# Softmax attention: probabilities scaled in place and transposed, instead of multiplied with a diagonal matrix

## The chip, the cores and the metric

The kernel runs on one core of one Trainium2 chip, as one program. The metric is device microseconds of one execution. A core has five engines that each run their instructions in order and meet only through semaphores: PE (matrix products, with PEld for the load of the stationary operand), DVE and ACT (elementwise work, reductions, functions, and copies out of PSUM), POOL, and SP, which here issues the transfers from memory.

## The reference, cut to what matters

Two layers of a first block and two of a second one, on 512 tokens of width 1024, in 32-bit floats. The first block has four groups of four heads: softmax attention with forget gates (fox), latent attention (mla), stick-breaking attention, and a sliding window of 128 keys (swa). The second has eight heads of softmax attention over keys that an indexer picks (dsa), and two recurrent groups (rwkv, gdn). Each block also has dense projections and feed-forwards of width 2816. What the change touches is the same in fox, mla, swa and dsa:

```
s = jnp.einsum('bqhd,bkhd->bhqk', qi, k).astype(jnp.float32) * scale
...
p = jax.nn.softmax(s, axis=-1).astype(v.dtype)
return jnp.einsum('bhqk,bkhd->bqhd', p, v)
```

## The kernel before

Features lie on the 128 partitions and the 512 tokens along the free dimension (`x` is eight tiles of 128x512). Dense products run as three products of split 32-bit numbers (`mm3`: high times high, high times low, low times high, in the type float32r). Weights come by SP, are split by ACT (line 235) and by DVE or POOL (line 236), and stream through PE.

Attention works on pairs of heads and tiles of 128 queries. `pair` (line 641) is one query tile `i` of two heads, in stages separated by `yield`:

- the scores go to PSUM (`sc`); DVE adds the bias and takes the row's extreme in one pass (line 654), which gives the tile `p` in SBUF, 128 queries by n*128 keys. n is 1 to 4 for fox, mla and dsa, and 1 or 2 for swa;
- ACT takes the exponential in place and adds up the row (line 665);
- DVE takes one over the row's sum (line 672), and the identity is multiplied by it, per partition, into a 128x128 tile `dg` (line 674, through `lin`). For head 0 in the first block (site `dg0`, listed in `ACT`) that is ACT at line 107, for head 1 there and for both heads in the second block DVE at line 109;
- PE multiplies each 128x128 block of `p`, as the stationary operand, with `dg` (line 681, through `mm`, line 164). This turns the block and divides it by the row's sum at once. The results lie in PSUM (`pt`) and are copied to SBUF (`pT`, line 682);
- PE multiplies the values with `pT` into `ot`, and ACT copies that out (lines 687 and 688).

There are 24 such pairs in each layer of the first block (8 each of swa, fox and mla) and 16 in each layer of the second. Per layer they have, over both heads, 108 blocks of 128x128 in the first block (28 swa, 40 fox, 40 mla) and 80 in the second: 376 in the whole kernel.

The order on PE is written ahead of time by `weave`: each stream (a pair, a recurrence, the projections as filling) yields an estimate of PE time until its next stage can start, and the stream that has been ready longest is written next. The clock of this planner, `self.t`, grows by an estimate for each product: in `mm` 4/2400 us for each column of a 32-bit float (0.213 us for 128 columns), in `tr` 0.21 us for a transpose. Three pairs are in flight at a time (`L1`, `L2`). The transposes of the kernel before, such as those of the dsa queries (`qqp`) and of the recurrences' matrices (`iXT`), go through `tr`, line 168.

Of the kernel before, what the change touches and what calls it, by code (L numbers as in the profile page):

```python
# [17 lines left out]
T = 512  # L18
D = 1024
# [47 lines left out]
class Ctx:  # L67
# [36 lines left out]
    def lin(self, site, out, x, scale, bias=0.0):  # L104
        """out = x scale + bias"""
        if site in ACT:
            self.nc.scalar.activation(out, x, AF.Identity, scale=scale, bias=bias)
        elif isinstance(bias, float) and bias == 0.0:
            self.nc.vector.tensor_scalar(out, x, scale, None, op0=OP.mult)
        else:  # L110
            self.nc.vector.tensor_scalar(out, x, scale, bias, op0=OP.mult, op1=OP.add)
# [5 lines left out]
    # interleaved emission ------------------------------------------------------------  # L117
    # A stream is a generator. It yields the tensor engine's time (us) until its next stage can start, or a key
    # that some other stream announces with done or hit. Engines run in order, so the streams are merged by
    # this clock: the stage that has been ready for longest comes next, and fill streams where none is ready.  # L120
# [30 lines left out]
    @staticmethod  # L151
    def lanes(gens, n):
        """n streams that share the generators of a list in order"""
        it = iter(gens)

        def lane():
            for g in it:
                yield from g
        return [lane() for _ in range(n)]
# [10 lines left out]
    # tiles ---------------------------------------------------------------------------  # L170
# [15 lines left out]
    def tables(self, k):  # L186
        """loads the activation engine's set of functions k, here in its order"""
# [20 lines left out]
    def split(self, src, name, w=T, gain=None):  # L208
        """hi + lo == src (times gain) exactly, both exact in float32r"""
# [10 lines left out]
    # dense products ------------------------------------------------------------------  # L220
    def weight(self, src, nk, m, name="w", eng=None, slots=False):
        """split weights [(hi, lo)] of nk k tiles [128, m]; slots: in the tiles of S instead of the weights' own"""
# [27 lines left out]
    def dense(self, jobs, head=0, ws=()):  # L250
        """jobs (weights, k tiles, columns, run(split weights)) in order, the weights ahead; ws = first split weights"""
# [9 lines left out]
    def tjob(self, src, nk, m, xs, fin, wait=None, name="pj"):  # L261
        """fin(psum [m, 512]) of weights^T times the transposed stream"""
# [13 lines left out]
    def kjobs(self, src, ncol, tiles, xs, fin):  # L276
        """token-major projections of at most four token tiles: x stationary, weights moving"""
# [19 lines left out]
    def part(self, E, p):  # L297
        """announces part p of the mixed features; project takes them in this order"""
        E["parts"].append(p)
        self.done.add("part%d" % len(E["parts"]))  # L300

    def heads(self, wgu):
        """the first weights of the next feed-forward, ahead of time"""
        self.head = {f: self.gateup(wgu, f) for f in range(HEAD)}

    def lead(self, srcs, nk, m, name, more=False):
        """the first weights of the next projections, ahead of time"""
# [6 lines left out]
    def project(self, E, src, xd, parts, scale, st, mean, last, wgu):  # L314
        """x = scale x + (mixed features)^T w, part by part: parts[p] = first k tile, splits(); last(j) when x[j] is done"""
# [27 lines left out]
    def gemmx(self, a, b, w, xs):  # L343
        """weights^T times a presplit stream: tokens of the first half to a, second half, gains and biases to b"""
# [4 lines left out]
    def unpack(self, a, b, eng, name):  # L349
        """the products of gemmx: tile [128, 512] and columns g W, b W"""  # L350
# [20 lines left out]
    # norms ---------------------------------------------------------------------------  # L371
    def sums(self, st, x, j, mean=True):
        """running sums over the feature tiles of the transposed stream (or of some of its tokens)"""
# [17 lines left out]
    def colstats(self, st, mean, tag="d"):  # L391
        """per token tile columns: mean square [, mean]"""
# [7 lines left out]
    def rows(self, col, ps=None):  # L400
        """[128 tok, n] -> PSUM [128, n * 128], every partition the row over tokens"""
# [6 lines left out]
    def hcol(self, sqs, col):  # L408
        """sums of squares over the two heads of each tile: PSUM [128 tok, 8 per tile = 4 token tiles x 2]"""
# [6 lines left out]
    def hrows(self, m, i):  # L416
        """columns of tile i -> PSUM [128 = 2 heads x 64, 512 tok]"""
# [7 lines left out]
    def rsqrt(self, y, a, scale=1.0):  # L425
        """y = scale / sqrt(a) for small tiles: Newton from an estimate in the bits of the float"""
# [10 lines left out]
    def rs_col(self, ps, eps, w):  # L437
        """1 / sqrt(ps + eps)"""
# [5 lines left out]
    # LayerNorm(x) W = r (x g) W - r mean (g W) + b W: the first products run on (x g) and take r and the mean later.  # L444
    def lngain(self, gcol, bcol, f=None):
        """g and the splits [128, 8, 4] of g and b per feature tile (hi, hi, lo, lo), all times f"""
# [14 lines left out]
    def presplit(self, x, j, gains):  # L461
        """the split of x g, with the gains and biases as two more columns"""
# [9 lines left out]
    def unfold(self, t, rows, m):  # L472
        """t (x g) W -> LayerNorm(x) W in place; m = columns g W, b W"""
# [7 lines left out]
    def lnrows(self, st):  # L481
        """rows r and -mean r over the tokens, in two steps"""
# [15 lines left out]
    def ln(self, x, rows, gcol, bcol, split, each=None):  # L498
        """LayerNorm over features of x (in place), split if asked for; each(x[j], j) as they come. In steps."""
# [26 lines left out]
    def gnorm(self, ts, n, gcols, name, out):  # L526
        """rms norm of a group of n features held transposed in the tiles ts; out gets the splits"""
# [21 lines left out]
    def swiglu(self, xs, wgu, wdn, evac, stats, ahead, finish=None, npre=0):  # L549
        """evac(half, j, psum) takes tile j of the halves of the down projection. stats = steps to the rows of the norm;  # L550
        with finish, xs is presplit, and finish(rows) -> split of the normalized stream, the steps of its own rows or
        None. The steps of the norm go between the first products."""
# [87 lines left out]
    # softmax attention ---------------------------------------------------------------  # L640
    def pair(self, wait, score, vget, bias, i, first, out, fin, sinks=None, dg="dg", pt="pT", pace=PACE1):
        """query tile i of two heads -> out [128 = 2 x 64 dv, 128 q] in SBUF, from softmax of -(negs + bias).
        score(h, i, first, n, ps) fills the negated logits; vget(h, key tile) -> [128 keys, 64]."""
# [23 lines left out]
        ds = []  # L667
        for h in range(2):
            m = ms[h]
# [3 lines left out]
            d = self.S("dg", w=128)  # L673
            self.lin(dg + str(h), d, self.ident, m[:, 2:3])
            ds.append(d)
        yield pace[2]
        pts = []
        for h in range(2):
            t = self.P("pt", w=w)
            for j in range(n):  # L680
                self.mm(t[:, j * 128:(j + 1) * 128], ps[h][:, j * 128:(j + 1) * 128], ds[h])
# [9 lines left out]
    # block 1 -------------------------------------------------------------------------  # L691
# [31 lines left out]
    def block1(self, l, x, xs, pre, a):  # L723
        """pre: None or presplit stream before its norm, its sums, finish(rows) -> x, xs"""
# [301 lines left out]
    # block 2 ------------------------------------------------------------------------  # L1026
    def rms(self, st, tag="d", rtag="o"):
        """1/rms per token, in two steps: per token tile [128, 4], and broadcast over partitions [128, 512]"""
# [4 lines left out]
    def ffn(self, x, xs, st, wgu, wdn, gnext, ahead, finish=None):  # L1033
        """x + swiglu(rms norm of x) / 2 from its split and its sums; the split for the next gains, and the sums"""
# [12 lines left out]
    # delta rules: units u = (pair, chunk, head of the pair); chunks of 128 tokens --------  # L1047
# [11 lines left out]
    def diag16(self, X, n, Y):  # L1059
        """X: 4 tiles [128, 4 units, 128], strictly upper; the list Y gets tiles with (I - X)^-1 of the 16 x 16  # L1060
        diagonal blocks, zero elsewhere."""
# [25 lines left out]
    def merges(self, X, Y, RH, fin):  # L1087
        """Y from inverses of diagonal 16 blocks to (I - X)^-1 for the 4 units of X [128, 4, 128];
        fin takes [128, 2 chunks, (u | w) x 2 heads x 64] = inverse times the right-hand side RH"""
# [60 lines left out]
    def gram(self, p, cp, lts, rts, outs):  # L1150
        """outs[m] [128 s, 4 units, 128 t] = lts[m]^T rts[m] per head and chunk of the pair p, chunks 2cp, 2cp+1,
        each given as (destination [128, 4, 128], factor [128, 4, 128] or [128, 128])"""
# [14 lines left out]
    def tokmajor(self, srcs, p, cp):  # L1167
        """transposes of the pair tiles' chunks 2cp, 2cp+1: PSUM [128 tok, src, chunk, 128 (2 heads x 64)]"""
# [7 lines left out]
    def step(self, ch, St, UW, kd, M, dst, qg, ediag, fscale, extra=None):  # L1176
        """outputs of chunk ch (over qg's columns, in place) and the next block-diagonal state St[0].
        UW [128, 256] = u (2 heads x 64) | w (2 heads x 64); kd [128, 128]; M(e) [128 s, 128 t]"""
# [52 lines left out]
    def rwkv(self, l, vec, E):  # L1231
        """projected tiles r0..r6 = wl, r, r, k, k, v, v, each [128, 513] with a zero column first."""
# [219 lines left out]
    def gdn(self, l, vec, E):  # L1452
        """projected tiles g0..g5 = q q k k v v [128, 515] with 3 zero columns first; z0, z1; ba [128 tok, 4, 8]."""
# [31 lines left out]
        def rowpair(name, p, k):  # L1485
            """row k (0: summed gates, 1: beta) of the pair's heads: [128 = 2 heads x 64, 512 tok]"""
# [155 lines left out]
    # sparse attention -------------------------------------------------------------------  # L1642
    def rope(self, x, ct, st, nh, out, tag):
        """token-major rotation of [128, nh, 64]; ct, st [128, 64]."""
# [11 lines left out]
    def headnorm(self, x, nh, scale):  # L1656
        """[128, nh] of scale / rms over each head of 64."""
# [10 lines left out]
    def stacked(self, src, name, out):  # L1668
        """[128 tok, 8 heads, 64] -> two float32r tiles [128 = hi 64 | lo 64, 4 heads, 128 tok]"""
# [68 lines left out]
    def logits(self, ps, q, g, n):  # L1738
        """two float32r passes over [hi; lo] stacked queries: q [128, 128], keys of head g"""
# [206 lines left out]
def pack_t(w, nk):  # L1946
    """[K, N] -> [N/128, 128, nk*128] with feature k*128 + p on partition p."""
# [4 lines left out]
def pack_dn(w):  # L1952
    """[F, D] -> [2, 8, 128, 11*128]"""
# [214 lines left out]
```

## Time and profile before

| what | value |
|---|---|
| three runs | 3784.54, 3784.54 and 3778.14 us; median 3784.54 us |
| profiled execution, first to last instruction | 3779.7 us; what lies around it is not shown |
| PE busy in it | 3683.6 us (97%) |
| DVE, ACT, POOL busy | 2093.9 us (55%), 1439.4 us (38%), 288.5 us (8%) |
| mean granted clock of PE | 0.987 of full speed |
| products into `pt`: PE records, summed busy time | 752, 100.5 us |

PE's records overlap, and their ends are modelled, so the summed busy time of PE is more than the time it takes; what an instruction costs is read from one start to the next. POOL's spans are rough. Attention of the first block lies at about 31 to 285 us and 731 to 985 us of the span, the dsa pairs at about 2066 to 2150 us and 3266 to 3350 us. What lies between is mostly feed-forwards.

### The profile page before, as it was taken

The numbers are of one execution on the slowest core, as the hardware profiler recorded it, in microseconds if no ns is written. First come the engines' busy times: TensorE is split into PE (matmuls) and PEld (weight loads), VectorE is DVE, ScalarE is ACT, GpSimd is POOL, SyncE is SP. The second block draws the span as 40 slices with busy tenths as digits, with TensorE's granted clock in tenths as the row PEclk, the third lists the DMA queues.
The fourth block names the chain that finished last, engine by engine and source line by source line (L and its number), as shares of the span: only waits on it lengthen the run. The fifth ranks groups of instructions, "written<-read, shape, count | busy, mean of one in ns | idle before, by whom it ended". The sixth has DMA issues, their size and how long they took to land.

```text
span 3779.7 us, 49398 instructions
## 1 busy us (share of the span) xinstructions
PE 3683.6 (97%) x19004; PEld 2980.8 (79%) x19004; DVE 2093.9 (55%) x4405; ACT 1439.4 (38%) x2706; POOL 288.5 (8%) x294
## 2 busy tenths in 40 slices
PE   9999999999999999999998999999999999899999
PEld 7777888777788888888786878888888777688887
DVE  5378333647653357345699564444444678855343
ACT  5455222545442235223443542233223433543222
POOL 1111000111200000001212000000000211100000
PEclk9999999999999999999998999999999999899999
DMA  3113232211223232324212132323233321213332
GB/s 127 47 57 102 84 106 86 94 61 48 86 88 98 88 96 88 102 87 144 76 54 65 39 101 85 105 87 99 85 103 99 95 69 50 79 33 102 95 95 89
DMA packets 146843, 320.72 MB, mean 85 GB/s; under 512 B 31496, under 2 KB 57768, under 8 KB 146352
## 3 DMA queue, kind: packets, MB, share of 16 engines
q1 hardware_dynamic: 146608, 317.57, 27.3%
q8 instruction: 149, 2.44, 0.3%
q14 instruction: 86, 0.70, 0.1%
HBM read 301.74 MB, written 15.78 MB: 84 GB/s over the span
## 4 chain that ended last, share of the span: by engine, by line
PE 87%; DVE 9%; ACT 1%; issue 1%; DMA 1%; POOL 0%; DVEq 0%; ACTq 0%; POOLq 0%
PE gup L164 37%; PE dn L164 19%; PE pjp L164 6%; PE wop L164 3%; PE tp L164 3%; PE pt L164 2%; PE sc L164 2%; PE ot L164 1%; PE gux L164 1%; PE iY L164 1%; PE G L164 1%; PE iR L164 1%; DVE isc L1778 1%; PE rowp L164 1%; PE sb L164 1%
## 5 line engine op out<-in xcount | busy, mean ns | idle before, releaser
L164 PE MATMUL dn<-hh,downl 128*128 128x512 f32 x1056 | 416.5, 394 | 0.0
L164 PE MATMUL dn<-hh,downh 128*128 128x512 f32 x1056 | 416.0, 394 | 0.0
L164 PE MATMUL dn<-hl,downh 128*128 128x512 f32 x1056 | 415.8, 394 | 0.0
L164 PE MATMUL gup<-xsh,gh 128*128 128x512 f32 x976 | 385.3, 395 | 0.7 <-ACT xsh L216 0.6
L164 PE MATMUL gup<-xsl,gh 128*128 128x512 f32 x976 | 385.3, 395 | 0.2 <-DVE xsl L217 0.2
L164 PE MATMUL gup<-xsl,uh 128*128 128x512 f32 x976 | 385.1, 395 | 0.0
L164 PE MATMUL gup<-xsh,uh 128*128 128x512 f32 x976 | 384.8, 394 | 0.0
L164 PE MATMUL gup<-xsh,ul 128*128 128x512 f32 x976 | 384.6, 394 | 0.0
L164 PE MATMUL gup<-xsh,gl 128*128 128x512 f32 x976 | 384.6, 394 | 0.0
L235 ACT CAST downh<-down 128x768 fp32r<-128x768 f32 x192 | 150.0, 782 | 518.6 <-PE dn L164 316.2
L597 DVE TENSOR_TENSOR hh<-gup,silu 128x512 f32<-128x512 f32 x122 | 84.4, 692 | 398.8 <-PE gup L164 393.2
L235 ACT CAST gh<-g 128x1024 fp32r<-128x1024 f32 (+1 forms) x138 | 139.2, 1013 | 415.2 <-issue 325.8
L236 DVE TENSOR_TENSOR downl<-down,downh 128x768 fp32r<-128x768 f32 x192 | 171.3, 893 | 217.7 <-ACT downh L235 216.6
L235 ACT CAST uh<-u 128x1024 fp32r<-128x1024 f32 (+1 forms) x138 | 139.4, 1012 | 354.9 <-PE gup L164 319.7
L236 DVE TENSOR_TENSOR ul<-u,uh 128x1024 fp32r<-128x1024 f32 (+1 forms) x138 | 162.3, 1178 | 152.3 <-ACT uh L235 148.4
L164 PEld LDWEIGHTS dn<-hl,downh 128*128 128x128 f32 x1056 | 198.3, 188 | 47.1
L164 PEld LDWEIGHTS dn<-hh,downl 128*128 128x128 f32 x1056 | 198.2, 188 | 46.7
L164 PEld LDWEIGHTS dn<-hh,downh 128*128 128x128 f32 x1056 | 198.3, 188 | 46.4
L164 PEld LDWEIGHTS gup<-xsh,gh 128*128 128x128 f32 x976 | 183.3, 188 | 44.7 <-ACT xsh L216 1.7
L164 PEld LDWEIGHTS gup<-xsl,gh 128*128 128x128 f32 x976 | 183.3, 188 | 44.5 <-DVE xsl L217 1.2
L164 PEld LDWEIGHTS gup<-xsh,uh 128*128 128x128 f32 x976 | 183.3, 188 | 43.5
L164 PEld LDWEIGHTS gup<-xsh,ul 128*128 128x128 f32 x976 | 183.3, 188 | 43.1
(595 smaller groups left out, 7473.3 us busy)
## 6 DMA issues: line engine op xcount, KB each, us to landing
g<-in_w_gu_dram SPq DMA_DIRECT2D x132, 512.0 KB, 3.5
u<-in_w_gu_dram SPq DMA_DIRECT2D x132, 512.0 KB, 3.5
down<-in_w_dn_dram SPq DMA_DIRECT2D x96, 384.0 KB, 3.1
pj<-in_w_in_dram SPq DMA_DIRECT2D x62, 512.0 KB, 3.7
down<-in_w_dn_dram SPq DMA_DIRECT2D x96, 320.0 KB, 2.9
wo<-in_w_o_dram SPq DMA_DIRECT2D x96, 128.0 KB, 2.2
xd<-x SPq DMA_DIRECT2D x24, 256.0 KB, 2.0
x<-xd SPq DMA_DIRECT2D x24, 256.0 KB, 5.0
```

The costliest lines, as they stand in the source:

```text
L164: self.nc.tensor.matmul(out, l, r, start=start, stop=stop)
L235: nc.scalar.copy(hi, r)
L236: (eng or nc.vector).tensor_sub(lo, r, hi.bitcast(F32))
L597: nc.vector.tensor_mul(hh, u, s)
L1778: nc.vector.match_replace(acc, m8, acc, -2.0 * BIG)
```

## The change

The 128x128 diagonal is no longer made. Instead the probabilities themselves, 128 by n*128, are multiplied by one over their row's sum, in place, by the same engine that made the diagonal. PE then transposes each block with the identity. The copies, the products with the values and the sites that choose the engines stay. The diff also takes comments and docstrings out of the file; all else of it is here:

```
         yield pace[1]
-        ds = []
         for h in range(2):
-            m = ms[h]
+            m, p = ms[h], ps[h]
             if sinks is not None:
                 nc.vector.tensor_add(m[:, 1:2], m[:, 1:2], m[:, 3:4])
             nc.vector.reciprocal(m[:, 2:3], m[:, 1:2])
-            d = self.S("dg", w=128)
-            self.lin(dg + str(h), d, self.ident, m[:, 2:3])
-            ds.append(d)
+            self.lin(dg + str(h), p, p, m[:, 2:3])
         yield pace[2]
         pts = []
         for h in range(2):
             t = self.P("pt", w=w)
             for j in range(n):
-                self.mm(t[:, j * 128:(j + 1) * 128], ps[h][:, j * 128:(j + 1) * 128], ds[h])
+                self.tr(t[:, j * 128:(j + 1) * 128], ps[h][:, j * 128:(j + 1) * 128])
             pts.append(self.evac(t, "a" if h == 0 else self.o(pt), name="pT"))
```

## Rows read from the trace of the kernel before

**Rows 1.** The page: busy time per engine, then the chain that ended last.

```profile
PE 3683.6 (97%) x19004; PEld 2980.8 (79%) x19004; DVE 2093.9 (55%) x4405; ACT 1439.4 (38%) x2706; POOL 288.5 (8%) x294
...
PE 87%; DVE 9%; ACT 1%; issue 1%; DMA 1%; POOL 0%; DVEq 0%; ACTq 0%; POOLq 0%
```

**Rows 2.** Windows: window, us, busy us per engine (x instructions), PEclk, DMA share, GB/s.

```profile
31.00:80.00 49.00, 47.61 (x311) 38.71 (x310) 28.90 (x132) 27.98 (x88) 4.77 (x2) 1.00 0.11 33
130.00:200.00 70.00, 70.00 (x401) 49.97 (x401) 37.76 (x114) 38.34 (x107) 8.53 (x11) 1.00 0.04 12
200.00:285.00 85.00, 83.44 (x486) 62.42 (x485) 63.63 (x172) 49.91 (x137) 13.29 (x20) 1.00 0.21 63
...
2066.00:2092.00 26.00, 24.99 (x165) 20.13 (x164) 23.27 (x101) 17.99 (x67) 3.45 (x3) 1.00 0.49 147
2092.00:2165.00 73.00, 73.00 (x656) 63.85 (x656) 33.06 (x101) 41.48 (x107) 1.27 (x1) 1.00 0.11 32
```

**Rows 3.** The same windows, instructions on the tile pt alone.

```profile
31.00:80.00 49.00, 7.56 (x56) 7.17 (x56) 3.11 (x8) 2.74 (x8) 1.00 0.11 33
130.00:200.00 70.00, 10.69 (x80) 9.78 (x80) 3.93 (x8) 3.34 (x8) 1.00 0.04 12
200.00:285.00 85.00, 10.26 (x80) 10.10 (x80) 3.78 (x8) 3.39 (x8) 1.00 0.21 63
...
2066.00:2092.00 26.00, 6.88 (x48) 6.15 (x49) 0.00 (x0) 4.39 (x16) 1.00 0.49 147
2092.00:2165.00 73.00, 14.38 (x112) 13.31 (x112) 0.00 (x0) 8.44 (x17) 1.00 0.11 32
```

**Rows 4.** Groups by form: into pt, into iXT, copies out: busy us, mean ns | idle before.

```profile
L164 PE MATMUL pt<-dg,p 128*128 128x128 f32 x752 | 100.5, 280 | 3.8 <-DVE dg L109 3.3 <-ACT pT L194 0.4
...
L168 PE MATMUL iXT<-cs,X 128*128 128x128 f32 x64 | 8.4, 275 | 0.0
...
L194 ACT COPY pT<-pt 128x512 f32<-128x512 f32 x24 | 13.9, 581 | 10.6 <-PE pt L164 10.5
...
L194 ACT COPY iXT<-iXT 128x512 f32<-128x512 f32 x16 | 8.6, 595 | 0.1
```

**Rows 5.** Timeline of PE, clock 1.00: start us, us, instruction, xcount.

```profile
2097.24 1.50 PE L164 MATMUL pt<-dg,p 128*128 128x128 f32 x12
2098.58 1.47 PE L168 MATMUL iXT<-cs,X 128*128 128x128 f32 x12
2099.89 0.84 PE L164 MATMUL pt<-dg,p 128*128 128x128 f32 x6
```

**Rows 6.** ACT groups by form: the diagonal, and exponentials with one value a partition.

```profile
L665 ACT ACTIVATE p<-p,m 128x256 f32<-128x256 f32 x56 | 28.0, 500 | 5.3 <-DVE m L654 5.2
...
L665 ACT ACTIVATE p<-p,m 128x512 f32<-128x512 f32 x32 | 23.1, 722 | 10.8 <-DVE m L654 10.7
...
L107 ACT ACTIVATE dg<-cs,m 128x128 f32<-128x128 f32 x48 | 18.0, 395 | 0.5 <-DVE m L672 0.5
```

**Rows 7.** DVE, tiles dg and kk: duration ns min/median/max of a multiplication.

```profile
L109 DVE TENSOR_SCALAR dg<-cs,m x112: 266/283/1135, 37.0 to 3339.1; 128x128 f32<-128x128 f32 x112
L109 DVE TENSOR_SCALAR kk<-sh,vec x4: 486/961/1436, 1818.1 to 3010.6; 128x512 f32<-128x512 f32 x4
```

**Rows 8.** Waits of PE over the span: waited for, us in total, times, longest us.

```profile
PE pt L164 <- DVE dg L109: 3.3, 5, 1.2
```

**Rows 9.** Timeline of PE around the transposes of the queries, second layer.

```profile
3259.26 0.63 PE L164 MATMUL wop<-mxh,woh 128*128 128x512 f32 x1
3259.68 3.38 PE L168 MATMUL qqp<-cs,qqs 128*128 128x128 f32 x16
3262.82 0.48 PE L164 MATMUL wop<-mxl,woh 128*128 128x512 f32 x1
...
3264.02 2.12 PE L168 MATMUL qqp<-cs,qqs 128*128 128x128 f32 x16 [0.27 <-ACT qqt L194]
3265.97 0.50 PE L164 MATMUL sc<-kst,qqt 128*128 128x256 f32 x2
```

**Rows 10.** Windows there: all engines, then PEclk.

```profile
3252.50:3255.90 3.40, 1.34 (x6) 0.75 (x4) 3.40 (x28) 1.11 (x3) 1.74 (x2) 0.99 0.01 2
3255.90:3259.20 3.30, 1.39 (x3) 1.16 (x4) 3.30 (x12) 0.72 (x3) 1.59 (x2) 0.50 0.00 0
3259.20:3262.60 3.40, 3.40 (x16) 2.96 (x15) 3.24 (x12) 0.71 (x2) 1.68 (x1) 0.50 0.00 0
3262.80:3266.00 3.20, 2.93 (x23) 2.19 (x21) 2.58 (x9) 3.20 (x8) 0.00 (x0) 1.00 0.78 259
```

More of the change, by code (lines that the diff above doesn't have):

```diff
@@ L666, in pair @@
         yield pace[1]
-        ds = []
         for h in range(2):
-            m = ms[h]
+            m, p = ms[h], ps[h]
             if sinks is not None:
@@ L672, in pair @@
             nc.vector.reciprocal(m[:, 2:3], m[:, 1:2])
-            d = self.S("dg", w=128)
-            self.lin(dg + str(h), d, self.ident, m[:, 2:3])
-            ds.append(d)
+            self.lin(dg + str(h), p, p, m[:, 2:3])
         yield pace[2]
@@ L680, in pair @@
             for j in range(n):
-                self.mm(t[:, j * 128:(j + 1) * 128], ps[h][:, j * 128:(j + 1) * 128], ds[h])
+                self.tr(t[:, j * 128:(j + 1) * 128], ps[h][:, j * 128:(j + 1) * 128])
             pts.append(self.evac(t, "a" if h == 0 else self.o(pt), name="pT"))
```

## The prediction

> **What bounds the kernel now.** I read the page first: PE is busy 97% of the span, and 87% of the chain that ended last runs through PE [rows 1]. That is an average over unlike stages, so the next view is the windows in which the pairs lie. PE fills the windows 130 to 200 us and 2092 to 2165 us without a gap; it has 1.4 us free of 49 in the first attention window and 1.6 of 85 in the third. In the first dsa window it has 1.0 free of 26, but there DVE is busy for 23.3 us of 26 and PE follows it [rows 2]. The windows of the other layers (731 to 985 us and 3266 to 3365 us) repeat these five. Then I looked at whether PE ever stands still for the thing that changes: over the whole span it waits for a finished diagonal 3.3 us, in 5 places [rows 8]. So the diagonals are nearly always early, and what counts is what the products themselves take on PE.
>
> **What one block costs on PE, before and after.** The busy times of PE's groups overlap (280 ns a product's record, 275 ns a transpose's [rows 4]), and by them the two cost the same. Two other readings say otherwise. One is the number of records: the code has 376 blocks, and `pt` has 752 matmul records, two for each block; `iXT` goes through `tr`, its 16 copies of 512 columns make 64 blocks of 128, and it has 64 records, one for each [rows 4]. A product of plain 32-bit floats is run as two passes and a transpose as one. The other is the distance of starts, where 12 records of each kind stand side by side at full clock: the 12 of `pt` take 2098.58 - 2097.24 = 1.34 us, 112 ns each, and the 12 transposes 2099.89 - 2098.58 = 1.31 us, 109 ns each [rows 5]. A block costs 2 x 112 = 224 ns as a product and 109 ns as a transpose of the same 32-bit type. The saving is 115 ns a block, 376 x 0.115 = 43.2 us. By stretch, with half the records of [rows 3] as blocks: 28, 40 and 40 blocks in the three windows of the first block (3.2, 4.6 and 4.6 us), 24 and 56 in the two of the second (2.8 and 6.4 us), each twice.
>
> **What is added.** The reciprocal is multiplied into 128 to 512 columns where it was into 128. On ACT (48 times) a multiplication of 128 columns takes 395 ns. For wider ones I take the exponentials, which have the same form: 500 ns for 256, 722 ns for 512 and the middle, 611 ns, for 384 [rows 6]. With 12, 20, 8 and 8 of the four widths that is 20 x 0.105 + 8 x 0.216 + 8 x 0.327 = 6.4 us. On DVE (112 times) 128 columns take 283 ns in the median, and the same operation on 512 columns takes 486 ns at its shortest [rows 7], so 68 ns for each further block: 20 x 0.068 + 8 x 0.135 + 8 x 0.203 = 4.1 us in the first block, and 16 x (0.068 + 0.135 + 0.203) = 6.5 us in the second, where both heads use DVE. These 17 us lie on engines that are half to three fifths busy in three of the five windows, in front of products that hardly ever wait. From below the price on the path is nothing (the cover is other work on PE). From above, with all cover gone, it is the longer of the two engines for each pair: 6.4 us in the first block and 6.5 us in the second, 13 us. I take 1.5 us, near the lower end because of the 3.3 us of [rows 8]: 0.5 us in each first dsa window, where DVE is full and 8 multiplications have one block more, and 0.5 us elsewhere. The diagonals' tiles fall away, which frees small tiles and costs nothing. Behind a longer multiplication on ACT stand exponentials and copies of other pairs, on DVE also the splits of weights. That is the same cover, in the same bound.
>
> **How much of the saving stays.** The order on PE is fixed in advance, and the planner takes 0.21 us for a transpose and took 0.213 us for a product. So the order stays almost as it is, while a transpose really takes 109 ns. Wherever one pair's blocks were to cover another pair's wait, up to 0.1 us of cover a block is gone, 0.8 us for a pair with n = 4. What can then be late is `ot`, which needs both copies of `pt`, 0.58 us each at full width [rows 4], or the score of another pair. The bounds are nothing kept and 43.2 us kept. By window:
>
> - 31 to 80 us: PE already waits a little and the chain passes over DVE and ACT. I keep 2.0 of 3.2 us.
> - 130 to 200 us: no gap, DVE and ACT half busy. 4.0 of 4.6.
> - 200 to 285 us: DVE is 75% busy. 3.9 of 4.6.
> - 2066 to 2092 us: DVE sets the pace. 0.7 of 2.8.
> - 2092 to 2165 us: no gap, DVE 45% busy, and the recurrences' products, which do not change, cover the pairs. 5.5 of 6.4.
>
> The sum is 16.1 us, twice 32.2 us. Less 1.5 us for the multiplications, and 1.5 us for a stretch or two more at the half clock when PE stands still more often, it leaves 29 us. Against the profiled execution's span, 3779.7 us, that is 3750.7 us. The median of the runs is 4.8 us above that span (the fastest run is 1.6 us below it), and with this offset the prediction is 3755.5 us.
>
> **The clock, a rule that speaks against the change.** In the second layer PE stood nearly still from 3252.5 to 3255.9 us, then its granted clock was 0.50, that is 1.2 of 2.4 GHz, until 3262.6 us, and from 3262.8 us it was 1.00 again [rows 10]. Between 3259.68 us and that rise PE ran 16 transposes in a row, 196 ns each. The next 16, from 3264.02 us, took 122 ns each, at full clock [rows 9]. So the clock rose out of a stretch that was nearly all transposes, and stayed up through another. The Trainium skill (TensorE: Matmul & The Clock Gate, Part 4: PE-mode transpose) says that the full clock does not engage for transposes, because they do not count as activity the way products do. By that rule transposes would not have brought this rise; the trace disagrees with it.
>
> **The rivals.**
>
> 1. The forecast, 0.60: 3748 to 3764 us.
> 2. All of it stays, 0.15: what PE's order covers is enough everywhere, 3784.5 - 43.2 = 3741 us. For it: no group waits for the diagonals now. Against it: the DVE-bound windows.
> 3. Most of it turns into other waits, 0.14: only the two gapless windows (130 to 200 and 2092 to 2165 us) keep two thirds, 2 x 7.3 = 14.6 us, 3770 us. For it: the planner's estimate is now twice the real time. Against it: four windows have idle time on DVE and ACT.
> 4. The multiplications become the wait, 0.05: DVE's 512-column form took up to 1.44 us beside 0.49 us [rows 7], 0.95 us more where something held it up. There are 84 multiplications on DVE wider than one block. Were 31 of them held up and exposed, the 29 us would be gone and the time 3784.5 us; with all of them it would be 3835 us. Against it: the mean of the narrow ones is 313 ns and few of the 112 are long.
> 5. Slower through the clock, 0.05: if PE drops to its half clock wherever the pairs' transposes stand, each of the 376 takes another 109 ns, 41 us, and the time is 3784.5 - 29 + 41 = 3796 us. It decides from 58 us at half clock on, since each us there loses half a us; the five windows, twice, have 606 us. Speaking for it is only that the clock does fall in these layers when PE is idle. This is what the rule of the Trainium skill named above would do.
> 6. The change does nothing, 0.01: transposes of probabilities stand as two records as well. Then it saves 376 x 6 ns = 2 us, 3782 us. All transposes of 32-bit floats in the trace have one.
>
> **How the numbers follow.** The likeliest is 3755.5 us, 0.77% less. The range goes from rival 2 to rival 3, 3741 to 3772 us, and leaves out rivals 4 to 6 and the outer ends. A difference of 0.2%, 7.6 us, is about what a measurement of this kernel can tell from none, so faster means under 3777 us: rivals 1 to 3, 0.89. Within 0.2%: most of 4, and 6, 0.06. Slower: 5, less where it is mild, and the far end of 4, 0.05.
>
> **What will show it.** The group into `pt` has 376 matmul records at line 168 instead of 752 at line 164, and 109 ns between them. The multiplications have four forms, about 0.28 to 0.49 us on DVE and 0.40 to 0.72 us on ACT. The windows' work ends earlier: the attention of each first-block layer by about 10 us, the dsa pairs by about 6 us, and the feed-forwards between them last as long as before. The waits of PE for `p` and `pT` grow by a few us in all. The prediction is wrong if PE's waits grow by more than 20 us, if the mean granted clock falls under 0.98, or if copies or scores, not multiplications, turn out to stand before PE.

## The result, and the profile after

The changed kernel took 3739.5 us (median of four runs, 3738.5 to 3745.3) beside 3781.3 us for the kernel before: a ratio of 0.9892, with a 95% interval of 0.9880 to 0.9904. Run again on another chip it took 3739.8 us (3736.8 to 3740.4) beside 3782.0: 0.9889 (0.9874 to 0.9904). That is 41 to 42 us less. The forecast was 29 us less, and 3755.5 us, with a range that ended at 3741. The direction was right and the size was not. The number of rival 2, "all of it stays" (3741 us), came out nearly, but not by its reason, as the stages below show.

The page of the changed kernel, busy time per engine and the chain that ended last, as in [rows 1]:

```profile
PE 3644.6 (97%) x18628; PEld 2936.3 (78%) x18628; DVE 2103.4 (56%) x4405; ACT 1443.8 (39%) x2706; POOL 289.8 (8%) x294
...
PE 88%; DVE 9%; ACT 1%; issue 1%; DMA 1%; POOL 0%; DVEq 0%; ACTq 0%; POOLq 0%
```

PE has exactly 376 instructions fewer (19004 to 18628), DVE and ACT as many as before. DVE is busy 9.5 us longer, ACT 4.4 us, and PE 39 us less.

The groups by form that answer to [rows 4, 6, 7]; the tiles `dg` are gone, and the multiplications stand as `p<-p,m`:

```profile
L168 PE MATMUL pt<-cs,p 128*128 128x128 f32 x376 | 57.4, 283 | 3.5 <-DVE p L109 2.4 <-ACT iXT L194 0.4 <-ACT pT L194 0.3
...
L109 DVE TENSOR_SCALAR p<-p,m 128x256 f32<-128x256 f32 x36 | 13.3, 376 | 0.4
L109 DVE TENSOR_SCALAR p<-p,m 128x512 f32<-128x512 f32 x24 | 12.3, 523 | 0.5
...
L107 ACT ACTIVATE p<-p,m 128x256 f32<-128x256 f32 x20 | 10.0, 499 | 0.5 <-DVE m L670 0.5
L107 ACT ACTIVATE p<-p,m 128x512 f32<-128x512 f32 x8 | 5.8, 723 | 0.0
```

A block has one record where it had two. The record's own length did not change (283 ns beside 280), which is why that column could not price the change: the records of a group overlap, and their starts lie closer than their lengths. ACT's wide multiplications took what the exponentials had told, 499 and 723 ns (500 and 722 assumed). DVE's took 376 and 523 ns, a little more than the 351 and 486 assumed.

Waits of PE over the span, as in [rows 8]: waited for, us in total, times, longest us.

```profile
PE rowp L164 <- DVE rsc L433: 5.5, 3, 2.5
PE pt L168 <- DVE p L109: 2.4, 4, 0.9
PE pt L168 <- ACT iXT L194: 0.4, 1, 0.4
PE pt L168 <- ACT pT L194: 0.3, 1, 0.3
PE ot L164 <- ACT pT L194: 0.3, 1, 0.3
PE pt L168 <- DVE m L654: 0.2, 1, 0.2
```

The kernel before has this row in front of the norm's product `rowp`, the one that spreads the norm's factors over the partitions:

```profile
PE rowp L164 <- DVE rsc L433: 1.7, 3, 1.0
```

The waits in front of `pt` and `ot` come to 3.6 us in 8 places; before, they were 3.7 us in 6. All waits of PE together went from 90.9 us in 81 places to 93.7 us in 77 (95.0 us in 79 in the repeated execution); the wait in front of `rowp` alone grew by 3.8 us. The forecast had taken 11 of the 43.2 us for lost, most of it as new waits.

The windows that answer to [rows 2], with ends moved to the same work; columns as there:

```profile
31.00:80.00 49.00, 48.89 (x301) 38.55 (x300) 31.14 (x137) 30.10 (x89) 4.92 (x3) 1.00 0.13 44
130.00:200.00 70.00, 70.00 (x362) 46.97 (x363) 38.84 (x113) 39.35 (x106) 8.78 (x12) 0.93 0.04 12
200.00:281.00 81.00, 80.07 (x446) 58.33 (x445) 63.10 (x171) 50.17 (x136) 13.14 (x20) 0.98 0.21 66
```

PE is as full as before. Two of the three show a granted clock below 1.00, which they did not have before; this execution, at a mean clock of 0.985, was the slowest of the four. In the repeated one (span 3737.9 us, clock 0.988, close to the 0.987 of the profiled execution of before) the stages can be compared better. I cut both traces at the same instructions: the first product of the attention and the first of the feed-forward's norm in each layer of the first block, the transposes of the dsa queries and the first of the norm behind them in the second. All engines, the kernel before:

```profile
31.90:320.80 288.90, 278.92 (x1565) 211.26 (x1564) 177.46 (x502) 151.63 (x387) 49.78 (x48) 1.00 0.19 58
320.80:684.30 363.50, 363.50 (x1684) 298.86 (x1683) 160.35 (x236) 121.11 (x163) 9.12 (x6) 1.00 0.32 95
684.30:1021.30 337.00, 317.55 (x1772) 244.81 (x1772) 211.31 (x560) 175.44 (x423) 58.33 (x57) 0.97 0.21 67
1021.30:2058.80 1037.50, 1015.63 (x5195) 838.12 (x5193) 601.59 (x1177) 371.82 (x602) 73.52 (x76) 0.98 0.29 88
2058.80:2217.20 158.40, 155.78 (x1142) 129.05 (x1142) 104.07 (x315) 88.49 (x229) 13.49 (x12) 0.99 0.24 71
2217.20:3259.70 1042.50, 1012.23 (x4856) 816.71 (x4855) 575.00 (x1099) 334.36 (x536) 65.79 (x76) 0.98 0.28 86
3259.70:3415.90 156.20, 154.37 (x1139) 129.62 (x1139) 100.79 (x300) 88.32 (x229) 13.20 (x12) 0.99 0.23 70
```

The same seven stages of the changed kernel, repeated execution:

```profile
32.40:312.00 279.60, 268.99 (x1459) 198.79 (x1457) 180.34 (x502) 154.13 (x387) 50.09 (x48) 0.99 0.19 60
312.00:677.10 365.10, 365.10 (x1684) 300.29 (x1683) 160.40 (x236) 121.22 (x163) 9.09 (x6) 1.00 0.31 94
677.10:1002.00 324.90, 305.73 (x1664) 230.63 (x1663) 213.00 (x560) 178.34 (x423) 58.06 (x57) 0.97 0.22 70
1002.00:2032.80 1030.80, 1008.53 (x5195) 832.80 (x5193) 600.89 (x1177) 371.99 (x602) 74.14 (x76) 0.99 0.28 89
2032.80:2185.70 152.90, 148.90 (x1058) 120.97 (x1059) 105.22 (x315) 87.64 (x229) 12.96 (x12) 0.98 0.23 72
2185.70:3225.30 1039.60, 1008.61 (x4858) 816.46 (x4856) 577.07 (x1099) 334.23 (x536) 67.84 (x76) 0.98 0.28 87
3225.30:3373.70 148.40, 145.00 (x1061) 118.42 (x1060) 102.88 (x300) 87.14 (x229) 13.23 (x12) 1.00 0.24 74
```

The changes are -9.3, +1.6, -12.1, -6.7, -5.5, -2.9 and -7.8 us; the two ends of the span add 0.9, in all -41.8 us. The four stages that hold the pairs gave 34.7 us. The 1037.5 us between the blocks gave 6.7 us, though nothing was changed there: PE ran 5195 instructions in both and stood still for 21.9 and 22.3 us, but it was busy 7.1 us less, and the clock's records show 25.1 us at half clock there instead of 38.6.

One execution against one can mislead, so here are eight profiles, cut at the same instructions. In the first four PE runs products in the first block, in the last four transposes; the experiments are described below. Each entry is us, with the us at half clock in brackets:

| first block | kernel | layer 1 | layer 2 | between the blocks |
|---|---|---|---|---|
| products | before | 288.9 (0.0) | 336.9 (17.1) | 1037.5 (38.6) |
| products | scaled in place, products | 289.1 (6.8) | 334.6 (17.1) | 1037.8 (38.6) |
| products | the new count, products | 291.6 (6.8) | 334.1 (13.7) | 1034.5 (31.9) |
| products | the change in the second block only | 294.8 (10.2) | 335.3 (13.7) | 1034.5 (31.9) |
| transposes | the change | 284.7 (20.5) | 328.2 (27.3) | 1030.3 (25.1) |
| transposes | the change with the old count | 280.0 (6.8) | 323.7 (20.5) | 1030.9 (20.0) |
| transposes | the change in the first block only | 278.1 (0.0) | 323.0 (17.1) | 1031.2 (20.0) |
| transposes | the change, again | 279.6 (3.4) | 324.9 (20.5) | 1030.8 (25.1) |

In the means layer 1 is 10.5 us shorter, layer 2 is 10.3 and the stretch between the blocks 5.3. In all ten profiles with transposes in the first block that stretch took 1026.7 to 1033.4 us, with 20.0 to 28.4 us at half clock; in the four with products it took 1034.5 to 1037.8 us, with 31.9 to 38.6.

### The profile page after: what moved, and what is told of

Read it like the earlier page. It is cut to its first block, busy times and chain, and to the rows that moved or that the text cites. A ratio compares the mean times of both kernels' runs of the same rounds, so it can differ in the third digit from the quotient of the medians.

```text
span 3743.6 us, 48619 instructions
## 1 busy us (share of the span) xinstructions
PE 3644.6 (97%) x18628; PEld 2936.3 (78%) x18628; DVE 2103.4 (56%) x4405; ACT 1443.8 (39%) x2706; POOL 289.8 (8%) x294
## 4 chain that ended last, share of the span: by engine, by line
PE 88%; DVE 9%; ACT 1%; issue 1%; DMA 1%; POOL 0%; DVEq 0%; ACTq 0%; POOLq 0%
PE gup L164 37%; PE dn L164 19%; PE pjp L164 7%; PE wop L164 4%; PE tp L164 3%; PE sc L164 2%; PE ot L164 1%; PE pt L168 1%; PE gux L164 1%; PE iY L164 1%; PE iR L164 1%; PE G L164 1%; PE rowp L164 1%; PE sb L164 1%; DVE isc L1775 1%
## 5 line engine op out<-in xcount | busy, mean ns | idle before, releaser
L235 ACT CAST gh<-g 128x1024 fp32r<-128x1024 f32 (+1 forms) x138 | 139.3, 1014 | 412.2 <-issue 324.9
L164 PEld LDWEIGHTS gup<-xsl,uh 128*128 128x128 f32 x976 | 183.2, 188 | 43.0
```

The costliest lines, as they stand in the source:

```text
L164: self.nc.tensor.matmul(out, l, r, start=start, stop=stop)
L235: nc.scalar.copy(hi, r)
```

## The experiments

The first theory says that PE keeps all that it saves, 115 ns a block, since it nearly never waits for a pair. The forecast's own view is its rival: a part of the saving turns into other waits, because the order written by the planner covers less. Each kernel was timed in turn with the kernel before on one chip. A ratio is turned into us with 3780 us.

**The longer multiplications without the transposes.** The probabilities are scaled in place, but still multiplied with the plain identity.

```
-                self.tr(t[:, j * 128:(j + 1) * 128], ps[h][:, j * 128:(j + 1) * 128])
+                self.mm(t[:, j * 128:(j + 1) * 128], ps[h][:, j * 128:(j + 1) * 128], self.ident)
```

> The longer multiplication alone: the probabilities are scaled in place as in the change, and PE still runs a product, with the identity, so the planner's clock and PE's order are those of before. Theory 1 (PE's own time is all that counts here, and slack in front of the products hides the rest): no change, 0 to +2 us. Theory 2 (the forecast's losses are real: the longer multiplications become waits): +3 to +13 us. Theory 3 (the new order on PE brought a part of the gain): no statement, as theory 1.

3779.3 us, 0.9994 (0.9986 to 1.0003): 2 us less, and not told from none. The scaling alone costs nothing that can be measured, and PE's waits for it are one row:

```profile
PE pt L164 <- DVE p L109: 0.8, 2, 0.6
```

**The change in the old order.** The planner counts a transpose of probabilities as it counted the product.

```
                 self.tr(t[:, j * 128:(j + 1) * 128], ps[h][:, j * 128:(j + 1) * 128])
+                self.t += 128 * 4 / 2400.0 - 0.21
```

> The change, but the planner counts each transpose as the product it replaces (0.2133 us), so that the stages stand in the order of before. Theory 1: the same 41 us faster as the change, 0.988 to 0.990 of before, within 4 us of the change. Theory 2: as the change. Theory 3 (order): only 29 to 35 us faster, 0.991 to 0.9925, since the rest came from the order that the smaller count brought.

3742.8 us, 0.9898 (0.9884 to 0.9911), 39 us less. In the trace this is nearly the old order in the dsa pairs, and only there. In the first block PE's order is that of the change in every place (records into one tile that follow each other counted as one), and it differs from the kernel before in 41 places.

**The new order without the change.** The products with the diagonal stay, and the planner counts 0.21 us for each.

```
+                self.t += 0.21 - 128 * 4 / 2400.0
                 self.mm(t[:, j * 128:(j + 1) * 128], ps[h][:, j * 128:(j + 1) * 128], ds[h])
```

> The kernel before, with its products with the diagonal, but the planner counts each as 0.21 us, so that the stages stand in the order of the change. Theory 1: 0 plus or minus 3 us. Theory 3 (order): 6 to 12 us faster, 0.997 to 0.9985.

3778.2 us, 0.9993 (0.9984 to 1.0002). The 3 ns by which the planner's count differs move PE's order in some 60 places, which I had not expected, nearly all of them in the dsa pairs; in the first block the order is that of the kernel before in every place. So the two runs rule out the order as the source of the gain in the second block, and say nothing of the first, where the order of the change comes by something other than this count. For layer 1 there is other evidence: the kernel without the multiplication (below) has the order of before there, but for some single records that moved a little, and its transposes make that stage 278.3 us beside 289.1 in the kernel with the scaling and products, both with 6.8 us at half clock.

**Each block transposed twice.** The second transpose writes the same values to the same place.

```
                 self.tr(t[:, j * 128:(j + 1) * 128], ps[h][:, j * 128:(j + 1) * 128])
+                self.nc.tensor.transpose(t[:, j * 128:(j + 1) * 128], ps[h][:, j * 128:(j + 1) * 128], self.ident)
```

> The change, with each block transposed a second time into the same place, uncounted by the planner. Theory 1: the 376 extra transposes cost 376 x 109 ns = 41 us over the change, so that the kernel is as slow as before, 0.999 to 1.001. Theory 2 (PE has spare time at the pairs since other engines set the pace there): 25 to 33 us over the change, 0.9955 to 0.998.

3772.7 us, 0.9982 (0.9973 to 0.9991): 7 us under the kernel before, so the 376 added transposes cost about 34 us. Here the two lines alternate on PE, so that every record has its own start (us, us long, at full clock):

```profile
142.50 0.27 PE L679 MATMUL pt<-cs,p 128*128 128x128 f32 x1
142.60 0.27 PE L168 MATMUL pt<-cs,p 128*128 128x128 f32 x1
...
143.37 0.27 PE L679 MATMUL pt<-cs,p 128*128 128x128 f32 x1
```

From 142.50 to 143.37 us lie eight records, 109 ns each. At that price the added ones are 41 us. PE's waits are 86.8 us here, 7 to 8 us less than with single transposes (93.7 and 95.0), some 3 us of it in front of `rowp` (2.3 us instead of 5.5). That the added work filled waits fits the 34 measured, as 41 less 7. Neither expectation was exact.

**Without the multiplication.** The division by the row's sum is left out, and the output differs by that.

```
-            self.lin(dg + str(h), p, p, m[:, 2:3])
```

> The change without the multiplication by one over the row's sum (the kernel leaves that division out; the reciprocals are still taken). Theory 1 (slack in front of the products hides the multiplications): as the change, 0.988 to 0.990 of before. Theory 2 (they are partly exposed, as the forecast had it): 1.5 to 13 us faster than the change, 0.985 to 0.988.

3734.7 us, 0.9880 (0.9867 to 0.9893), 45 us less. The interval overlaps that of the change: the multiplications are worth about 4 us, with an error of some 7 us, and are not told from nothing.

**The change in the first block only.** swa, fox and mla are transposed, dsa keeps the diagonal.

```
+                o, b = t[:, j * 128:(j + 1) * 128], ps[h][:, j * 128:(j + 1) * 128]
+                self.tr(o, b) if dg == "dg" else self.mm(o, b, ds[h])
```

> The change in the first block's 216 blocks alone (swa, fox, mla); dsa keeps products with the diagonal. Theory 1 (the full 115 ns of each block stays): 24.8 us faster than before, 0.9934, with 4 us to either side. Theory 2 (the forecast's shares): 18 to 20 us, 0.995.

3754.6 us, 0.9934 (0.9922 to 0.9946), 25 us less, of 24.8 that PE's records save there. These windows answer to the first, third and fourth stage of before:

```profile
32.50:310.60 278.10, 267.47 (x1458) 197.82 (x1457) 180.33 (x502) 154.17 (x387) 50.00 (x48) 1.00 0.19 60
674.20:997.20 323.00, 304.15 (x1664) 229.97 (x1663) 213.25 (x560) 178.29 (x423) 58.21 (x57) 0.97 0.22 70
997.20:2028.40 1031.20, 1008.46 (x5195) 832.55 (x5194) 601.02 (x1177) 372.20 (x602) 74.21 (x76) 0.99 0.28 89
```

In this execution the time at half clock was as in before within these two attention stages, and they are 10.8 and 14.0 us shorter, 24.8 us in sum; the forecast gave them 9.9 each, 19.8. That the sum equals what the records save is luck: 14.0 is more than the 12.4 us of a layer's 108 blocks, and over the four profiles of each kind the two stages give 20.8 us. The stretch between the blocks is 6.3 us shorter here, without a change in it. It is so in every profile with transposes in the first block, so a part of the 25 us lies there and not in the pairs.

**The change in the second block only.** The same switch the other way, `dg == "d2"`.

> The change in the 160 blocks of dsa alone. Theory 1: 18.4 us faster than before, 0.9951, with 4 us to either side. Theory 2 (the forecast: DVE sets the pace in the first dsa window): 10 to 12 us, 0.997.

3768.9 us, 0.9964 (0.9952 to 0.9976), 14 us less (9 to 18), of 18.4. The two dsa stages:

```profile
2060.70:2211.90 151.20, 147.75 (x1058) 119.83 (x1059) 105.02 (x315) 87.82 (x229) 12.77 (x12) 0.99 0.23 73
3256.50:3405.00 148.50, 144.91 (x1059) 118.30 (x1059) 102.63 (x300) 87.19 (x229) 12.96 (x12) 1.00 0.24 74
```

They are 7.2 and 7.7 us shorter than in before (158.4 and 156.2). The forecast gave 6.2 each, the first theory 9.2: here the forecast is nearer.

**The change, again.** The changed kernel as it is, beside the next three on one chip.

> The change as it is, once more on one chip with the next three, so that its size is known to about 3 us. Theory 1 (all that PE saves stays, 376 blocks at 115 ns, 43.2 us, less what the DVE-paced dsa window gives up, 1 to 5 us): 38 to 43 us less than the kernel before. The forecast's discounts: 27 to 32 us less. The two halves measured apart gave 25.0 and 13.6 us, 38.6 in sum; if they get in each other's way, less than that sum.

3739.8 us, 0.9889 (0.9874 to 0.9904), 42 us. The halves make 38.6 us, within the errors of it. Nothing shows that they get in each other's way.

**The true time in the planner.** It counts 0.109 us for a transpose of probabilities.

```
+                self.t += 0.109 - 0.21
```

> The change, and the planner counts 0.109 us for a transpose of probabilities instead of 0.21 us, so that the streams come in another order. Theory 1 (PE is nearly gapless under either order): within 3 us of the change. The forecast's reason for its discounts (the planner's count leaves too little cover behind the transposes): with the true count what is still lost comes back, 2 to 5 us less than the change.

3746.1 us, 0.9909 (0.9892 to 0.9925): 6 us above the change on the same chip, with overlapping intervals, though each of its four runs is longer than each of the change. Neither expectation came out. PE's waits are 93.1 us, as with the wrong count (93.7 and 95.0), and those in front of `rowp` 6.0 us. So the truth in the planner won nothing back, and the reason that the forecast gave for its discounts, the wrong count, is not borne out.

**Rows as transposes too.** `rows` (line 405) turns columns that are spread over 128 with a product with the identity, 104 times in the kernel; that product becomes a transpose as well.

```
-            self.mm(ps[:, t * 128:t * 128 + 128], col[:, t:t + 1].to_broadcast([128, 128]), self.ident)
+            self.tr(ps[:, t * 128:t * 128 + 128], col[:, t:t + 1].to_broadcast([128, 128]))
```

> The change, and the 104 products of a repeated column with the identity that spread a norm's factors over the partitions (tile rowp, 208 records of 112 ns) become transposes as well. Theory 1: PE's time is the bound there too: another 104 x 115 ns = 12 us, 0.985 to 0.987 of before. Theory 2 (these stand behind a chain on DVE, PE waits for their input in places, and what follows them waits for copies): 3 to 6 us more than the change, 0.987 to 0.9885.

3735.5 us, 0.9882 (0.9868 to 0.9896), 3 to 4 us better than the change, not clearly told from it, where 104 x 115 ns would be 12 us. PE's waits are 100.3 us here.

**Rows, and the true time.** Both edits together.

> The change, the products with the identity in rows() as transposes too, and the planner's count of 0.109 us for the probabilities. Theory 1: the sum of the two parts measured alone, 2 to 7 us less than the change, 3732 to 3738 us. Rival: the rows are waited for and not computed on the path, so the two parts together give no more than the change, 3738 to 3742 us.

3730.4 us, 0.9866 (0.9851 to 0.9880): 51 us less than the kernel before and the fastest of all, 9 us under the change and more than either theory gave. Against the kernel with the true count alone, on the same chip, the intervals do not meet. PE has 104 instructions fewer than in the change (18628 to 18524). The larger of the two groups into `rowp` went from 144 records to 72 (group by form, as in [rows 4]), the other from 64 to 32:

```profile
L168 PE MATMUL rowp<-cs,rsc 128*128 128x128 f32 x72 | 11.1, 277 | 6.0 <-DVE rsc L433 6.0
```

At 115 ns the 104 are 12.0 us, of the 15.7 us between this kernel and the one with the true count alone. The rest may be the clock, which is not shown: this profile, of the fastest of the four runs, has 78.7 us at half clock, that of the true count alone 92.4, and the repeated change 93.7.

**dsa's first multiplication on ACT.** One more site in the list, as the first block has it.

```
-ACT = ('dg0', 'p2', 'qq')
+ACT = ('dg0', 'd20', 'p2', 'qq')
```

> The change, and in the dsa pairs the multiplication of head 0 is done by ACT instead of DVE, as in the first block. The multiplications, 0.27 to 0.49 us each on DVE, leave it for 16 pairs a layer, some 6 us of DVE a layer, of which the 8 narrow ones (about 2.5 us) lie in the DVE-paced first dsa window. If DVE sets the pace there: 1 to 2.5 us a layer less, 2 to 5 us less than the change. Theory that DVE is no limit there, or that ACT, 72% busy in that window, becomes one: no difference, or up to 4 us more.

3736.0 us, 0.9880 (0.9865 to 0.9895): 4 us under the change, as expected if DVE set the pace, but the intervals overlap. The stage was read directly, from the first dsa score to the same product of a later pair, for three kernels. The kernel before:

```profile
2065.20:2104.60 39.40, 38.39 (x279) 31.61 (x279) 30.61 (x130) 28.58 (x96) 3.45 (x3) 1.00 0.47 141
```

The change, repeated execution:

```profile
2039.10:2079.70 40.60, 38.09 (x248) 28.66 (x247) 31.49 (x131) 29.47 (x99) 2.82 (x3) 0.96 0.45 136
```

This kernel:

```profile
2038.40:2076.30 37.90, 35.02 (x248) 27.08 (x248) 28.74 (x118) 32.48 (x108) 2.76 (x3) 1.00 0.48 146
```

DVE has 2.7 us less to do and the stretch is 2.7 us shorter, but the change ran 3.4 us of it at half clock, worth up to 1.7 us, and in the second layer the same stretch was 1.2 us longer (39.2 to 40.4 us). So what sets the pace there is not settled.

## Why the prediction was wrong, point by point

**Right: the price of a block.** 376 records, and 109 ns between them where the clock is full. The reading that decided it, counting records and taking starts instead of busy times, held: 376 added transposes cost 34 us, and the scaling with products in place of transposes gained nothing. Rival 6 (nothing happens) is out.

**Nearly right: "How much of the saving stays", in the first block.** The forecast kept 2.0 + 4.0 + 3.9 us a layer, 19.8 us of 24.8. The two stages gave 20.8 us in the means of four profiles, 21.4 in the repeated execution and 24.8 in the kernel with the first block alone. In layer 1 the discount can be followed to a wait. The third run of products into `rowp`, in the kernel before:

```profile
83.47 1.13 PE L164 MATMUL rowp<-cs,rsc 128*128 128x128 f32 x8 [0.36 <-DVE rsc L433]
```

The same in the repeated execution of the change:

```profile
83.83 1.16 PE L164 MATMUL rowp<-cs,rsc 128*128 128x128 f32 x8 [2.49 <-DVE rsc L433]
```

They start 51.6 and 51.4 us after the first product of the attention: PE had less to do, but the factors from DVE came no sooner, so PE stood 2.1 us longer. In layer 2 the same wait went from 0.39 to 2.34 us; in each layer a wait of 1.0 to 1.2 us for a diagonal fell away. PE also ran eight more filling products (1.9 us) ahead of this point than before, so 2.0 of 3.2 us stayed there. From it to the fourth run into `rowp` 4.6 of 4.6 us stayed, and 4.1 of 4.6 from there to the fifth. The forecast had looked for such a wait in front of `ot` or of a score, where it did not come (in front of `pt` and `ot` 3.7 us before, 3.6 after), and it had blamed the planner's count, with whose correction the wait stayed at 2.49 us. Rival 3, in which most of the saving turns into waits, is out.

**Right: the same step in the second block.** 12.4 of 18.4 us were kept in the sum; 13.6 us were measured alone (9 to 18), and 14.9 in its stages. The stretch from the first dsa score, held to be paced by DVE, has 31 blocks, 3.6 us, and kept nothing in the first layer (39.4 us to 40.6, at most 1.7 of that by the clock) and 0.6 us in the second (39.8 to 39.2); the forecast said 0.7 of 2.8. Between that point and the end of the first layer's stage the gain was 6.6 us, where 5.5 of 6.4 was forecast. That DVE is the reason was argued and is not shown.

**Wrong, and the largest step that failed: the time outside the pairs.** The forecast put it at nothing ("the feed-forwards between them last as long as before") and the clock at a loss of 1.5 us. But the stretch between the blocks became 6.7 us shorter in the repeated execution and 5.3 in the means, with 13.5 us less at half clock and with the same PE instructions and idle time. It did so in each of the ten profiles with transposes in the first block. Why a change in the first block leaves less half clock behind it stays open; PE's order there changed with it in most of these kernels.

**Not borne out: 1.5 us for the clock.** I expected PE to stand still more often and lose time by it. Over the whole span half clock was 99.2 us in the profile of before and 114.1 and 93.7 in two profiles of the change; over the runs the mean clock was the same (0.988 before, 0.987 and 0.988 after). In the four stages with pairs it did grow, from 22.4 to 30.5 us in the repeated execution. Rival 5 would have needed 58 us more at half clock. The Trainium skill (TensorE: Matmul & The Clock Gate, Part 4: PE-mode transpose) says that the full clock does not engage for transposes; no run here shows it. With 752 transposes of probabilities half clock was 97.8 us, and those printed above, 109 ns each, ran at a clock of 1.00.

**Not told apart: 1.5 us for the multiplications.** Alone they changed the time by -2 us (-5 to +1); taken out of the change they gave about 4 us, with an error of 7. Both leave room for 1.5 us and none for the upper bound of 13. Rival 4 is out.

**Wrong: the base.** I added 4.8 us, the median less the profiled span. In every execution timed since, of any of the kernels, 1.7 to 1.8 us lie around the span. The other 3.0 us were only that the profiled execution was not one of the three timed ones, two of which were long ones among many: later medians of the kernel before were 3779.5 to 3782.0 us.

So of the 16 us by which 3755.5 was too high, 6.7 lie between the blocks, 3.0 are the base, 3.0 the deductions for multiplications and clock, 2.5 what the pairs' stages gave beyond the 32.2 us kept for them (34.7), and the rest the smaller stretches and rounding. That the total comes so near to 43.2 us, all that the records save, is luck: the pairs gave back 8.5 us of it, and the stretch between the blocks brought 6.7.

## What to carry to other kernels

Where a product with a diagonal only turns and scales a 32-bit tile, a transpose takes half of PE's time (109 against 224 ns for a block of 128), and in this kernel, where PE is the bound, the longer multiplications on other engines cost too little to be measured. The Trainium skill (Perfetto Trace Analysis, Optimizing Tensor Performance, Transposes) asks for real transposes in place of products, and this case agrees. To say how much of a saving stays, look behind it on the bounding engine for the next instruction whose input another engine delivers, and ask whether that input comes sooner: here the stretch in front of such a product lost 1.2 of 3.2 us, and the next one, in which PE never stood, kept all of its 4.6. And check the stretches that you did not touch in several executions before you book a time to the one that you changed.

## What the runs showed of the hardware that was not expected

**The clock's share of the scatter.** Over the 45 executions of the kernel before that were timed beside the experiments, the span goes with the mean granted clock: 3782.8 us on average at 0.986 (3 runs), 3778.3 at 0.988 (19), 3775.8 at 0.989 (10). Two executions of the changed kernel with 114.1 and 93.7 us at half clock (mean 0.985 and 0.988) have spans of 3743.6 and 3737.9 us: 20.4 us at half clock cost 5.7 us, less than half of them.

**The same wait, once with a fall of the clock behind it and once without.** Windows of the changed kernel, first profile, columns as before:

```profile
78.00:81.20 3.20, 2.79 (x13) 1.91 (x11) 3.00 (x7) 1.05 (x1) 1.34 (x1) 1.00 0.00 0
81.20:83.40 2.20, 0.12 (x1) 0.12 (x2) 1.85 (x6) 0.00 (x0) 1.02 (x1) 1.00 0.22 26
83.40:85.00 1.60, 1.60 (x13) 1.46 (x14) 0.53 (x1) 0.00 (x0) 0.00 (x0) 1.00 0.80 269
85.00:88.40 3.40, 3.40 (x9) 2.63 (x8) 2.97 (x8) 2.89 (x5) 0.00 (x0) 0.50 0.03 11
88.40:92.00 3.60, 3.60 (x22) 2.58 (x21) 1.01 (x2) 1.11 (x2) 0.00 (x0) 0.99 0.00 0
```

PE stood for 2.5 us in front of `rowp`, worked for 1.6 us at full clock, then had the clock at 0.50, 1.2 of 2.4 GHz, for 3.4 us of unbroken products, and 0.99 over the next 3.6 us. The repeated execution has the same wait of 2.49 us, and in the window behind it the clock stays at 1.00:

```profile
84.00:90.00 6.00, 6.00 (x33) 4.71 (x34) 3.67 (x9) 3.88 (x6) 0.00 (x0) 1.00 0.23 81
```

So a wait of this length does not settle whether the clock falls, and what does was not tried.
